# First block begun behind two quarters of the modulation, its columns in a fixed order, and small sums packed in column groups

## The chip, the core and the metric

The kernel runs on one core of a Trainium2 chip. The core has five engines, each with an instruction queue of its own: TensorE (PE) multiplies matrices and writes to PSUM banks, VectorE (DVE) and ScalarE (ACT) do element work, GpSimd (POOL) does small element work here, and SyncE (SP) issues the transfers (DMA) between the core's memory and HBM. Engines wait for one another through semaphores. The metric is the time of one execution on the device, in microseconds (us), lower is better; a time is the median of several executions.

## The reference

One layer of a diffusion backbone runs over 128 context tokens and 2048 latent tokens of width 1024. What the change touches is the beginning of the layer:

```
m = silu(cond) @ w_mod + b_mod                   # six vectors of 1024 for context and latent
h = rmsnorm(x, norm_mix) * (1 + sc1) + sh1       # modulated norm of the tokens
proj = h @ w_in                                  # q, k, v, gate, alpha/beta, u, vg
qkv = silu(centred_conv(proj[..., :1536], conv)) # three taps over neighbouring tokens
q, k = l2norm(q), l2norm(k)
beta2 = sigmoid(ab[..., 0]); g2 = -exp(a_log) * softplus(ab[..., 1] + dt_bias)
```

`ab`, the alpha and beta columns, are 16 of the 3088 columns of `w_in`. Behind it come a gated DeltaNet scan in two directions, a spatial gating, an output projection, a second modulated norm and an MLP.

## The kernel before

**Tiles and stages.** The 2176 tokens are 17 tiles of 128, in six blocks (`BLOCKS`): five of three tiles and a last one of two. Phase one goes over the blocks. The width 1024 is eight slices of 128, numbered `k` (`KT` = 8). A token block is kept transposed, features on the partitions, and split in two float32r halves, high and low, so that a product is three matrix products (`mm3`, L242 to L244): high by high, low by high, high by low.

**The modulation.** The first two of the six vectors are wanted at once. They are loaded as four quarters of eight loads of 256 KB (`mod_load`, L345): m0 and m2 are the halves of the shift, m1 and m3 those of the scale. `mod_sum` (L349) multiplies each slice's two columns of `scond` by the raw weights, in float32 and eight products in a row; `mod_out` (L358) turns the two rows into columns and makes `b1` (shift) and `a1` (scale and norm weight). Chunk `jc` = 4 of the later modulation is made by `split_mod_steps` (L372): each weight slice is split by ACT (a cast) and DVE (a subtraction) and multiplied with `abW`. The other chunks (`mod_steps`, L251) run on DVE, with a small packed sum at L281 at their end: there four products with two columns each go to PSUM partitions 0, 32, 64 and 96.

**A block.** `prep_block` (L446) yields steps: loading its x tiles, and one `column(k)` for each slice. For block 0 a column is three transposes on PE (L515), the modulation on ACT into `full` (L517), a cast to `kH` and a subtraction to `kL` on DVE (L520, L521), edge columns copied by POOL (L507 to L511) and four stores. Later blocks make `full` from transposed x on DVE (L527), `kH` on ACT and `kL` on DVE. The edges come from `xh`, the ten rows beside the block borders, normalised and modulated by `first_half` (L438) into `halH` and `halL`.

**A feature tile.** `feature_tile(blk, bi, gi, h)` (L545) is one of twelve in a block: group 1 is k, 0 is q, 2 is v, with four heads each. `project` does 24 products over the eight slices into a bank (`pj`, three of them; in block 0 one tile uses `pt`), then the convolution on ACT and DVE, then transposes back to tokens with squares for the norm (`to_tokens`, L582), back to features (L610) and the products of k and q (L620). `ab_block` (L638) multiplies the block's `kH` and `kL` with `abW`, which holds high and low halves of the alpha/beta weights (16 products), and transposes the 32 rows.

**What sets the order.** The kernel is written as lists of steps (`main` and `side`) which `interleave` merges; a scheduler then orders each engine's queue by its own estimate of times, within the dependences. `MOD_STEPS` says how many modulation steps go beside each tile of block 0. In block 0 (from L761 on) three k tiles are begun together on the first four columns; the fourth quarter is summed in between. Pools are rings of buffers: a new tile waits until an old one's last reader is done (`wp` has 49 of 2 KB on each partition, `full` two).

## Time and profile before

| | us |
|---|---|
| median of three executions | 2586.35 (2584.51 to 2587.87) |
| the profiled execution | 2589.03 |
| its span, first to last instruction | 2587.1 |
| PE busy in it | 2547.4 |
| PE busy from 0 to 100 us | 96.00 |
| first product of block 0 | at 36.87 |

The profile is one execution. Busy times are by engine; a row of the timeline gives start, length, engine, line, operation, what it writes and reads, its shapes and how many there are, and in brackets how long the engine stood idle before it and what ended that. A row of the table of stretches gives the stretch, its length and then, for PE, PE's weight loads (PEld), DVE, ACT and POOL, the busy time and (x) the instructions; then the granted clock of PE as a share of full speed, the mean share of the DMA engines and GB/s. A float32 product shows as two records. Rows of the chain of waits give start, length and what the chain that ended last went through.

### The profile page before, as it was taken

To read this page: it belongs to the slowest core of one execution; us is meant where nothing else is said; L and a number is where in the kernel's file an instruction comes from. 1 tells how busy PE (TensorE), PEld (TensorE's weight loads), DVE (VectorE), ACT (ScalarE), POOL (GpSimd) and SP (SyncE) were. 2 spreads that over 40 slices of the span, in tenths; PEclk is the share of its full clock that TensorE was granted. 3 is DMA by queue.
4 is the path that set the end of the run, shared out by engine and by line. 5 is a ranking of instruction groups with operands and counts; after the bars stand their busy time and mean duration, and the time that the engine had idled before them with its cause. 6 is when DMAs were issued, how large, how long until landed. Compare 5 with 4: busy or idle time off the path is not lost.

```text
span 2587.1 us, 44754 instructions
## 1 busy us (share of the span) xinstructions
PE 2547.4 (98%) x15556; PEld 2154.5 (83%) x15556; DVE 1805.3 (70%) x3738; ACT 1221.0 (47%) x3051; POOL 233.7 (9%) x448
## 2 busy tenths in 40 slices
PE   9999999999999999999999999999999999999998
PEld 5899998788888787788888888888888888888887
DVE  5867757766677878886678876666665557784875
ACT  4755556555555667764345543333342432342442
POOL 3112212111111111210000000000000000000000
PEclk9999999999999999999999999999999999999999
DMA  8977737644454656885868788444479979786683
GB/s 287 300 219 213 211 111 253 229 154 155 144 160 151 215 177 235 281 275 183 280 205 252 230 289 293 122 115 118 120 239 368 345 257 327 266 257 204 223 266 112
DMA packets 494695, 571.88 MB, mean 221 GB/s; under 512 B 35124, under 2 KB 297564, under 8 KB 490886
## 3 DMA queue, kind: packets, MB, share of 16 engines
q1 hardware_dynamic: 494470, 569.04, 67.8%
q8 instruction: 122, 2.00, 0.3%
q14 instruction: 103, 0.84, 0.1%
HBM read 389.23 MB, written 179.67 MB: 220 GB/s over the span
## 4 chain that ended last, share of the span: by engine, by line
PE 86%; DMA 6%; DVE 5%; ACT 2%; issue 1%; SPq 0%; POOL 0%; POOLq 0%; DVEq 0%; ACTq 0%
PE f L242 16%; PE f L244 16%; PE f L243 16%; PE pj L242 7%; PE pj L244 6%; PE pj L243 6%; PE pd L1011 4%; PE f L1646 2%; PE pm L242 1%; PE pm L244 1%; PE pm L243 1%; PE pt L626 1%; DMA QK<-qk_d 1%; DMA raw<-in_w_mod_dram 1%; DMA hop_d<-opL 1%
## 5 line engine op out<-in xcount | busy, mean ns | idle before, releaser
L242 PE MATMUL f<-hop,zH 128*128 128x512 f32 (+1 forms) x976 | 376.2, 386 | 1.2 <-ACT zH L1532 1.2
L243 PE MATMUL f<-hop,zH 128*128 128x512 f32 (+1 forms) x976 | 376.1, 386 | 0.0
L244 PE MATMUL f<-hop,zL 128*128 128x512 f32 (+1 forms) x976 | 376.1, 386 | 0.0
L242 PE MATMUL f<-hop,wH 128*128 128x512 f32 x896 | 355.2, 397 | 0.1
L243 PE MATMUL f<-hop,wH 128*128 128x512 f32 x896 | 349.0, 390 | 0.0
L244 PE MATMUL f<-hop,wL 128*128 128x512 f32 x896 | 347.9, 390 | 0.0
L1532 ACT CAST zH<-zraw 128x512 fp32r<-128x512 f32 x240 | 146.4, 620 | 284.6 <-DMA zraw<-s_d 86.9
L242 PEld LDWEIGHTS f<-hop,zH 128*128 128x128 f32 x976 | 183.3, 188 | 38.5 <-ACT zH L1532 1.6
L244 PEld LDWEIGHTS f<-hop,zL 128*128 128x128 f32 x976 | 183.3, 188 | 37.3 <-DVE zL L1526 0.4
L243 PEld LDWEIGHTS f<-hop,zH 128*128 128x128 f32 x976 | 183.3, 188 | 36.9 <-issue 0.2
L1526 DVE TENSOR_TENSOR zL<-zraw,zH 128x512 fp32r<-128x512 f32 x240 | 162.6, 687 | 72.2 <-ACT zH L1532 55.1
L244 PEld LDWEIGHTS f<-hop,wL 128*128 128x128 f32 x896 | 168.2, 188 | 35.3
L242 PEld LDWEIGHTS f<-hop,wH 128*128 128x128 f32 x896 | 168.5, 188 | 32.8 <-issue 0.5
L243 PEld LDWEIGHTS f<-hop,wH 128*128 128x128 f32 x896 | 168.5, 188 | 32.3
L242 PE MATMUL pj<-kH,wH 128*128 128x386 f32 (+2 forms) x568 | 190.5, 338 | 1.3 <-ACT junk L602 1.1
L243 PE MATMUL pj<-kL,wH 128*128 128x386 f32 (+2 forms) x568 | 189.5, 335 | 0.5 <-POOL kL L511 0.5
L244 PE MATMUL pj<-kH,wL 128*128 128x386 f32 (+2 forms) x568 | 189.7, 335 | 0.0
L185 POOL TENSOR_TENSOR r<-rsq,nhalf 128x1 f32<-128x1 f32 (+1 forms) x37 | 25.1, 679 | 1418.0 <-DVE rsq L184 1418.0
L572 DVE SCALAR_TENSOR_TENSOR cv<-pj,vec,cv 128x384 f32<-128x384 f32 (+2 forms) x164 | 87.0, 539 | 52.7 <-ACT cv L569 51.4
L242 PEld LDWEIGHTS pj<-kH,wH 128*128 128x128 f32 x568 | 107.0, 189 | 4.6 <-issue 2.6
L1532 ACT CAST wH<-s 128x512 fp32r<-128x512 f32 x96 | 59.4, 621 | 105.5 <-DVE s L1526 103.5
L243 PEld LDWEIGHTS pj<-kL,wH 128*128 128x128 f32 x568 | 107.4, 189 | 1.4 <-POOL kL L511 0.8
(410 smaller groups left out, 5703.9 us busy)
## 6 DMA issues: line engine op xcount, KB each, us to landing
zraw<-z_d SPq DMA_DIRECT2D x212, 256.0 KB
raw<-in_w_ff_dram SPq DMA_DIRECT2D x128, 256.0 KB
hop<-hop_d SPq DMA_DIRECT2D x28, 1024.0 KB
z_d<-c SPq DMA_DIRECT2D x96, 256.0 KB
zraw<-s_d SPq DMA_DIRECT2D x96, 256.0 KB
raw<-in_w_mod_dram SPq DMA_DIRECT2D x80, 256.0 KB
r<-in_w_ff_dram SPq DMA_DIRECT2D x80, 256.0 KB
s_d<-s SPq DMA_DIRECT2D x64, 256.0 KB
```

The lines of the kernel that those rows point to most:

```text
L185: G.tensor_tensor(out=out, in0=t[:np_, :n], in1=nhalf[:np_, :n], op=ALU.pow)
L242: T.matmul(ps, lh, rh, start=first and i == 0, stop=False, skip_group_check=more)
L243: T.matmul(ps, lh, rl, start=False, stop=False, skip_group_check=more)
L244: T.matmul(ps, ll, rh, start=False, stop=last and i == n - 1, skip_group_check=more)
L572: V.scalar_tensor_tensor(out=cv[:, o : o + m], in0=ps[:, s + sh : s + sh + m], scalar=convw[:, w, j : j + 1], in1=cv[:, o : o + m], op0=AL ...
L626: T.matmul(ps[:, i * P : (i + 1) * P], kTt[:, i * P : (i + 1) * P], rhs[:, i * P : (i + 1) * P], start=True, stop=True)
L1011: T.matmul(p[:, h, :], lhs[:, h, :], rhs[:, h, :], start=True, stop=True)
L1526: V.tensor_tensor(out=out, in0=a, in1=b, op=op)
L1532: A.copy(h, src)
L1646: T.matmul(ps[:, c : c + P], self.raw[m, kh][:, kp, :], x0[kh][:, kp, :], start=first and kp == 0, stop=last and kp == 3)
```

## The change

Quarters m0 and m1 are summed first, and then block 0 begins on columns 0 to 3 with four k tiles; m2 and m3 are summed between its slices (before slices 2 and 3), and columns 4 to 7 follow. The loads of x, the alpha/beta weights, the first two weight groups, m2 and m3 are issued in one chain on SP (`in_order`), and later loads of modulation and third weight group are put behind it (`follow`). PE's, DVE's and ACT's instructions from m1's sum to the end of slice 5 are chained in program order. `keep_on` puts 16 products of ones on PE behind m0's sum and 16 more behind the first edges. `first_half` works on four slices at once.

`groups` packs a sum over the eight slices: slice k goes to partitions 32 (k mod 4) of one bank, with 32 columns of `abW`, which now is float32 and holds alpha/beta in columns 0 to 15 and `scond` in 16 and 17. `sel` adds the four groups up in a further product. The four quarters, chunk 4, alpha/beta and a new `abias` (the shift's part of alpha/beta, for blocks 1 to 5) go through it. Alpha/beta is summed from `full` in float32, in two halves behind columns 3 and 7, so `full` has five buffers. The masks take another pool's room, and the zero edges of block 0 are written at the start.

```diff
-MOD_STEPS = (1, 1, 0, 0, 0, 1, 0, 2, 0, 1, 1, 2)
+MOD_STEPS = (0, 0, 0, 0, 1, 1, 0, 2, 1, 1, 2, 2)
...
-        abW = p1.tile([P, KT, P], F32R, tag="abW", name="abW", bufs=1)
-        V.tensor_copy(abW, zcol.unsqueeze(2).to_broadcast([P, KT, P]))
-        V.tensor_copy(abW[:, :, 32:34], scond)
-        V.tensor_tensor(out=abW[:, :, 64:66], in0=scond, in1=f32(abW)[:, :, 32:34], op=ALU.subtract)
+        abW = p1.tile([P, KT, 32], F32, tag="abW", name="abW", bufs=1)
+        V.memset(abW, 0.0)
+        V.tensor_copy(abW[:, :, 16:18], scond)
+        sel = p1.tile([P, 18], F32, tag="sel", name="sel", bufs=1)
+        V.tensor_tensor(out=sel, in0=ident[:, 0:18], in1=ident[:, 32:50], op=ALU.add)
+        for g in (64, 96):
+            V.tensor_tensor(out=sel, in0=sel, in1=ident[:, g : g + 18], op=ALU.add)
+        abias = p1.tile([P, 1], F32, tag="abias", name="abias", bufs=1)
+
+        def groups(ps, ks, moving):
+
+            for k in ks:
+                g = 32 * (k % 4)
+                T.matmul(ps[g : g + 32], abW[:, k, :], moving[k], start=k < 4, stop=k >= 4)
...
-            for k in range(KT):
-                T.matmul(pm[0:2, :], scond[:, k, :], raws[k], start=k == 0, stop=k == KT - 1)
-            row = pf.tile([2, 512], F32, tag="first", name="first", bufs=2)
-            A.copy(row, pm[0:2, :])
+            groups(pm, range(KT), raws)
+            row = pf.tile([P, 512], F32, tag="first", name="first", bufs=2)
+            A.copy(row, pm)
             return row
...
             for i in range(4):
-                T.transpose(pc[:, 2 * i : 2 * i + 2], row[:, i * P : (i + 1) * P], ident[0:2, 0:2])
+                T.matmul(pc[:, 2 * i : 2 * i + 2], row[:, i * P : (i + 1) * P], sel[:, 16:18], start=True, stop=True)
...
+                load(out=u[k], in_=w_mod[0, k * P : (k + 1) * P, jc * 512 : (jc + 1) * 512])
+                follow(start, loaded, mybir.EngineType.SP)
...
+                if i == 0:
+                    fetch(0), fetch(1), fetch(2), fetch(3)
+                elif i == 1:
+                    fetch(4), fetch(5)
+                elif i == 3:
...
+                    groups(u["ps"], range(4), u)
+                    in_order(begin, mybir.EngineType.PE)
+                    fetch(6), fetch(7)
+                    u["row"] = p1.tile([2, 512], F32, tag="mrow", name="mrow", bufs=1)
+                    load(out=u["row"], in_=b_mod[0:1, jc * 512 : (jc + 1) * 512].to_broadcast([2, 512]))
+                elif i == 6:
+                    groups(u["ps"], range(4, KT), u)
+                    in_order(begin, mybir.EngineType.PE)
+                    u["four"] = pf.tile([P, 512], F32, tag="first", name="four", bufs=2)
+                    A.copy(u["four"], u["ps"])
+                elif i == 7:
+                    ps = pm1()
+                    T.matmul(ps[0:2, :], sel[:, 16:18], u["four"], start=True, stop=True)
+                    V.tensor_tensor(out=u["row"], in0=ps[0:2, :], in1=u["row"], op=ALU.add)
+                    store(out=mod_d[:, jc * 512 : (jc + 1) * 512], in_=u["row"])
...
+        def follow(start, before, engine):
+
+            for x in tc.nc.cur_bb.bb.instructions[start:]:
+                if x.engine == engine:
+                    tc.add_manual_dep(x, before.name, mybir.DependencyInfo(
+                        mybir.DependencyClass.NoSync, mybir.DependencyReason.DATA), reason="order")
...
+        def in_order(start, *engines):
+
+            rows = tc.nc.cur_bb.bb.instructions
+            for e in engines:
+                own = [x for x in rows if x.engine == e]
+                at = len(own) - sum(x.engine == e for x in rows[start:])
+                for x, y in zip(own[max(at - 1, 0):], own[max(at, 1):]):
+                    tc.add_manual_dep(y, x.name, mybir.DependencyInfo(
+                        mybir.DependencyClass.NoSync, mybir.DependencyReason.DATA), reason="order")
...
+        def keep_on(n):
+
+            start, before = here(), last()
+            for _ in range(n):
+                T.matmul(warm[:, P : 2 * P], ones, ones, start=True, stop=True)
+            follow(start, before, mybir.EngineType.PE)
+
+        make_masks(pf.tile([P, 6, P], F16, tag="x2", name="one6", bufs=4))
+        edges = []
+        for k in range(KT):
+            pair = [p1.tile([P, 388], F32R, tag="h", name=n, bufs=24) for n in ("kH", "kL")]
+            for t in pair:
+                G.tensor_copy(t[:, 0:1], zcol[:, 0:1])
+                G.tensor_copy(t[:, 129:131], zcol[:, 0:2])
+            edges.append(pair)
...
         m0 = mod_load(0, 0)
         load(out=vec, in_=v_columns)
         convw = vec[:, 32:68].rearrange("p (w a) -> p w a", w=3)
+        xh = pf.tile([P, D], F32, tag="xh", name="xh", bufs=1)[0:10, :]
+        load(out=xh[0:8, :], in_=x_sample[0, 255 : 255 + 4 * 384, :].rearrange("(m r) d -> m r d", r=384)[:, 0:2, :])
+        load(out=xh[8:10, :], in_=x_sample[0, 255 + 384 * 4 : 257 + 384 * 4, :])
         m1 = mod_load(0, D)
+        start = here()
+        xs0 = []
+        for t in BLOCKS[0]:
+            x = p1.tile([P, D], F32, tag="x", name="x", bufs=3)
+            load(out=x, in_=xrow(t))
+            xs0.append(x)
+        abr = p1.tile([P, KT, 16], F32, tag="abr", name="abr", bufs=1)
+        load(out=abr, in_=w_ab)
+        w1a = load_w1(1, range(4))
+        m2 = mod_load(1, 0)
+        m3 = mod_load(1, D)
+        w1b = load_w1(1, range(4, KT))
+        wr = load_w1(0, range(KT))
+        in_order(start, mybir.EngineType.SP)
+        loaded = last()
         r0 = mod_sum(m0, pm1)
+        keep_on(2 * WARM)
+        pinned = here()
         r1 = mod_sum(m1, pj)
-        m2 = mod_load(1, 0)
+        def first_half(half):
+            ks = slice(half * 4, half * 4 + 4)
+            for tab, op in ((a1, ALU.mult), (b1, ALU.add)):
+                V.tensor_tensor(out=hal[:, ks, :], in0=hal[:, ks, :], in1=tab[:, 1, ks].unsqueeze(2)
+                                .to_broadcast([P, 4, 10]), op=op)
+            V.tensor_copy(halH[:, ks, :], hal[:, ks, :])
+            V.tensor_tensor(out=halL[:, ks, :], in0=hal[:, ks, :], in1=f32(halH)[:, ks, :], op=ALU.subtract)
+
         mod_out(r0, 0, b1, vec[:, 0:8], False)
...
-        r2 = mod_sum(m2, pj)
         norm_rows(xh)
...
-        xs0 = []
-        for t in BLOCKS[0]:
-            x = p1.tile([P, D], F32, tag="x", name="x", bufs=3)
-            load(out=x, in_=xrow(t))
-            xs0.append(x)
+        mod_out(r1, 0, a1, vec[:, 8:16], True)
+        first_half(0)
+        in_order(pinned, mybir.EngineType.PE, mybir.EngineType.DVE, mybir.EngineType.Activation)
+        keep_on(2 * WARM)
+        pinned = here()
         for x in xs0:
             norm_rows(x)
...
-                full = p1.tile([P, 384], F32, tag="full", name="full", bufs=2)
-                kH = p1.tile([P, 388], F32R, tag="h", name="kH", bufs=24)
-                kL = p1.tile([P, 388], F32R, tag="h", name="kL", bufs=24)
+                full = p1.tile([P, 384], F32, tag="full", name="full", bufs=5)
+                fulls[k] = full[:, :n]
+                if bi == 0:
+                    kH, kL = edges[k]
+                else:
+                    kH = p1.tile([P, 388], F32R, tag="h", name="kH", bufs=24)
+                    kL = p1.tile([P, 388], F32R, tag="h", name="kL", bufs=24)
...
+            def ab_sums(half):
+
+                if half == 0:
+                    sums["ps"] = pm1()
+                groups(sums["ps"][:, :n], range(4 * half, 4 * half + 4), fulls)
+                if half:
+                    sums["sb"] = sb = p1.tile([P, 384], F32, tag="absb", name="absb", bufs=1)
+                    if bi:
+                        V.tensor_scalar_add(sb[:, :n], sums["ps"][:, :n], abias)
+                    else:
+                        V.tensor_copy(sb[:, :n], sums["ps"][:, :n])
+
+            def ab_tokens():
+
+                pa = pt()
+                for i in range(len(tiles)):
+                    T.matmul(pa[:, i * 16 : (i + 1) * 16], sums["sb"][:, i * P : (i + 1) * P], sel[:, 0:16], start=True,
+                             stop=True)
+                V.tensor_copy(ab[:, tiles[0] : tiles[0] + len(tiles), :],
+                              pa[:, : len(tiles) * 16].rearrange("p (a b) -> p a b", b=16))
+
+            def column_sums(k, sums=True):
+                column(k)
+                if k % 4 == 3 and sums:
+                    ab_sums(k // 4)
+
...
+        def ab_bias():
+
+            ps = pm1()
+            groups(ps[:, 0:1], range(KT), [b1[:, 1, k : k + 1] for k in range(KT)])
+            V.tensor_copy(abias, ps[:, 0:1])
...
-        mods = [st for jc in range(4, 10) for st in (split_mod_steps(jc) if jc == 4 else mod_steps(jc, p1))]
+        mods = [st for jc in range(4, 10) for st in (group_mod_steps(jc) if jc == 4 else mod_steps(jc, p1))]
...
-        m3 = mod_load(1, D)
-        wr = load_w1(1, range(4))
-        mod_out(r1, 0, a1, vec[:, 8:16], True)
-        r3 = mod_sum(m3, pm1)
-        mod_out(r2, 1, b1, vec[:, 0:8], False)
-        W1[1] += [split_w(r) for r in wr]
-        first_half(0)
-        abr = p1.tile([P, KT, 16], F32, tag="abr", name="abr", bufs=1)
-        load(out=abr, in_=w_ab)
-        wk = load_w1(1, range(4, KT))
-        wr = load_w1(0, range(KT))
-        us = [feature_tile(blk, 0, 1, h) for h in range(3)]
-        for k in range(4):
-            cols[k]()
-            for u in us:
+        us = [feature_tile(blk, 0, 1, h) for h in range(4)]
+        cols[0](False)
+        W1[1].append(split_w(w1a[0]))
+        cols[1](False)
+        W1[1].append(split_w(w1a[1]))
+        for k in range(6):
+            if k == 3:
+                r3 = mod_sum(m3, pm1)
+                V.tensor_copy(abW[:, :, 0:16], abr)
+            for n, u in enumerate(us):
                 u["main"][k]()
-        mod_out(r3, 1, a1, vec[:, 8:16], True)
-        W1[1] += [split_w(r) for r in wk]
-        first_half(1)
-        for k in range(4, KT):
-            cols[k]()
-        V.tensor_copy(abW[:, :, 0:16], abr)
-        V.tensor_tensor(out=abW[:, :, 16:32], in0=abr, in1=f32(abW)[:, :, 0:16], op=ALU.subtract)
+                if n == 1 and k == 2:
+                    mod_out(r2, 1, b1, vec[:, 0:8], False)
+                if n == 1 and k == 3:
+                    mod_out(r3, 1, a1, vec[:, 8:16], True)
+                    first_half(1)
+                    cols[4](False)
+                    W1[1].append(split_w(w1b[0]))
+            if k == 1:
+                r2 = mod_sum(m2, pm1)
+            if k < 2:
+                cols[k + 2](False)
+                W1[1].append(split_w(w1a[k + 2]))
+            if k > 2:
+                cols[k + 2](False)
+                W1[1].append(split_w(w1b[k - 2]))
+            if k == 4:
+                blk[5](0)
+        blk[5](1)
+        in_order(pinned, mybir.EngineType.PE, mybir.EngineType.DVE, mybir.EngineType.Activation)
...
+        def third(k):
+            start = here()
+            raw = raw_w(w_in[0, k * P : (k + 1) * P, 1024:1536], sp, "raw")
+            follow(start, loaded, mybir.EngineType.SP)
+            W1[2].append(split_w(raw))
...
             if bi == 0:
-                order = [(1, 0), (1, 1), (1, 2), (0, 0), (0, 1), (1, 3), (0, 2), (0, 3)]
+                order = [(1, 0), (1, 1), (1, 2), (1, 3), (0, 0), (0, 1), (0, 2), (0, 3)]
...
-                main = u["main"][4:] if bi == 0 and n < 3 else u["main"]
+                main = u["main"][6:] if bi == 0 and n < 4 else u["main"]
...
-                if n == 1:
-                    ab1, ab2 = ab_block(blk, bi)
-                    side.append(ab1)
+                if bi == 0 and n == 1:
+                    side.append(ab_bias)
                 if n == 2:
-                    side.append(ab2)
+                    side.append(blk[4])
```

93 lines of the change are left out of this document (29 added, 64 removed).

## The prediction

> **What bounds the kernel now.** I read the page first (busy times, then the chain that ended last), then the table of stretches over the first 100 us, then TensorE's timeline there.
>
> ```profile
> PE 2547.4 (98%) x15556; PEld 2154.5 (83%) x15556; DVE 1805.3 (70%) x3738; ACT 1221.0 (47%) x3051; POOL 233.7 (9%) x448
> PE 86%; DMA 6%; DVE 5%; ACT 2%; issue 1%; SPq 0%; POOL 0%; POOLq 0%; DVEq 0%; ACTq 0%
> ```
>
> TensorE (PE) is busy for 98% of the span. So a microsecond is won where PE's own work shrinks or where PE is busy without getting on, and an idle PE has only 40 us to give in all. The start is the place of the second kind:
>
> ```profile
> 4.95 8.25 PE L353 MATMUL pm<-raw,scond 128*2 128x512 f32 x16
> 17.75 7.89 PE L353 MATMUL pj<-raw,scond 128*2 128x512 f32 x18
> 36.87 0.62 PE L242 MATMUL pj<-kH,wH 128*128 128x388 f32 x2
> 59.24 0.34 PE L242 MATMUL pj<-kH,wH 128*128 128x388 f32 x1
> 59.42 0.34 PE L243 MATMUL pj<-kL,wH 128*128 128x388 f32 x1
> ```
>
> The four modulation sums (L353) hold PE from 4.95 us until the first product of block 0 at 36.87: 8.25 us for a sum whose product appears as two records, so about 1 us a product. From there products follow one another every 0.18 us (59.24 to 59.42; I use 0.178).
>
> ```profile
> 49.53 0.45 PE L243 MATMUL pj<-kL,wH 128*128 128x388 f32 x1 [0.46 <-POOL kL L511]
> 70.67 0.52 PE L585 MATMUL pt<-ident,x 128*128 128x128 f32 x3 [0.76 <-DVE ab L657]
> 72.34 0.52 PE L585 MATMUL pt<-ident,x 128*128 128x128 f32 x3 [0.28 <-DVE x L576]
> 73.99 0.41 PE L242 MATMUL pj<-kH,wH 128*128 128x388 f32 x1 [1.13 <-ACT junk L602]
> 70.00:80.00 10.00, 7.93 (x46) 7.42 (x47) 9.31 (x27) 10.00 (x37) 1.27 (x2) 1.00 1.02 348
> ```
>
> After that PE stands 0.46 us once and 2.2 us around 72 us, where ACT is busy for all 10 us of its window (fourth engine column). There is little else to win in block 0.
>
> **When block 0 starts after the change.** The first product now needs quarters m0 and m1 alone, but it stands at the end of a chain that is pinned in program order on PE, DVE and ACT. Its links:
>
> ```profile
> 5.70 10.94 SPq L191 DMA_DIRECT2D raw<-in_w_mod_dram  x16
> 11.12 5.17 DMA raw<-in_w_mod_dram
> 20.53 0.57 ACT L355 COPY first<-pj 2x512 f32<-2x512 f32 x1 [6.72 <-PE pj L353]
> 22.89 1.05 ACT L336 ACTIVATE junk<-xh 10x1024 bf16<-10x1024 f32 x1 [1.78 <-DMA xh<-in_x_sample_dram]
> 25.54 0.13 DVE L184 TENSOR_SCALAR rsq<-ss 128x1 f32<-128x1 f32 x1
> 25.75 0.56 POOL L185 TENSOR_TENSOR r<-rsq,nhalf 128x1 f32<-128x1 f32 x1 [0.92 <-DVE rsq L184]
> 26.34 0.75 DVE L338 TENSOR_SCALAR x<-x,r 128x1024 f32<-128x1024 f32 x1 [0.67 <-POOL r L185]
> 27.72 0.66 PE L420 MATMUL pt<-ident,xh 10*128 10x10 f32 x8
> 29.52 0.23 DVE L421 COPY hal<-pt 128x80 f32<-128x80 f32 x1
> 156.70 0.67 PE pt L626 x6
> 28.03 0.22 DVE L369 SCALAR_TENSOR_TENSOR a<-a,vec 128x4 f32<-128x4 f32 x2
> 33.45 0.91 ACT L517 ACTIVATE full<-pt,b,a 128x128 f32<-128x128 f32 x2 [3.82 <-PE pt L515]
> ```
>
> The load issued at about 11.1 us, the sixteenth of 256 KB by SP's pace of 0.68 us (10.94/16), landed at 16.3; the two xh loads now ahead of m1 add some 0.6: 16.9. Then: last packed product 0.95 (17.85), copy of the sums 0.57 (18.4), square of xh 1.2 with its read-out (19.6), rsq, POOL's power and the scaling 1.55, that is 25.54 to 27.09 (21.2), xh's transposes and copy 0.9 (22.1), four 128-wide float32 products with sel at 0.22 each by L626's row (three products in 0.67) 0.9 (23.0), three small DVE steps 0.5 (23.5), four of first_half 0.7 at that pace (24.2). Only now may DVE take up the three x tiles, since its order is pinned, and each waits for POOL in turn: 3 x 1.55 = 4.65 (28.8). Transposes 0.33, ACT's pair 0.91, DVE's second cast 0.3: 30.4, with handovers **30.5 us**. Block 0 starts 6.4 us earlier. DMA doesn't bind: at 0.68 us a load, x, w_ab, four of w1, m2 and m3 have landed by 35, and their sums come behind it. If the chain of DVE were free, the last x tile (21 us) would give 25.3; if xh's small loads cost double, 31.1. The 16 filler products (keep_on, 3.6 us) end near 26.6 and hide behind this chain.
>
> **What block 0 then carries.** I compare the time at which the 96 products of tiles (1,0) to (1,3), the eight columns and the alpha/beta sums are through.
>
> ```profile
> 151.74 0.55 PE pm L281 x16
> 152.29 0.37 PE pj L242
> 152.66 0.17 PE pj L243
> 154.25 0.33 PE pt L585 x3
> 194.55 0.30 PE pt L654 x3
> 43.69 5.67 POOL L510 CAST kH<-halH 128x1 fp32r<-128x1 f32 x4 [8.83 <-DVE halH L443]
> L510 POOL CAST kH<-halH x32: 178/180/4917, 31.7 to 111.0; 128x1 fp32r<-128x1 f32 x32
> L520 DVE CAST kH<-full x16: 215/254/295, 33.9 to 51.7; 128x128 fp32r<-128x128 f32 x8, 128x256 fp32r<-128x256 f32 x8
> L202 ACT CAST wH<-raw x32: 606/622/787, 35.5 to 96.3; 128x512 fp32r<-128x512 f32 x32
> L203 DVE TENSOR_TENSOR wL<-raw,wH x32: 677/684/693, 36.2 to 96.9; 128x512 fp32r<-128x512 f32 x32
> ```
>
> L281 already packs columns: eight 128-wide products (16 records) pass in 0.55 us, against 8 x 0.22 one by one, 3.2 times as fast; the next product took 0.37, not 0.18, so a switch of tile shape costs 0.19. A 384-wide float32 product alone takes 0.75 x 0.99 = 0.74 us (0.99 is 7.89/8). Eight packed are 1.5 us if four lie wholly side by side, 1.85 at 3.2 times; I take 1.6, and 2.0 for 512 wide.
>
> Before: 36.87 + 96 x 0.178 (17.1) + 16 alpha/beta products (2.85) + seven columns' transposes at 0.33 (2.3) + four small transposes (0.4) + the 0.46 stall = 60.0. After: 30.5 + 17.1 + six columns (2.0) + the sums of m2 and m3 (4.0) + their collection with sel (1.8) + alpha/beta (1.6) + four switches (0.8) = 57.8, and four waits that the fixed order puts on PE:
> - wL of the first weight comes 0.4 late, behind column 0 on DVE.
> - Column 4 needs mod_out(r3) and first_half(1) first: about 0.8 beyond the products that cover it.
> - The sixth `full` finds no buffer (five) until ab_sums(0), which stands behind k = 4 on PE; then ACT's pair and DVE's cast, 1.5, and wL 0.5: 2.0. Nothing else can run on PE: three pj banks and the pt bank are held.
> - POOL's edge casts of columns 4 to 7. One took 4.9 us of the 5.67, while DVE had no gap. Between 0.2 and 4.9 us; behind the pinned order DVE has a gap after column 4 and its wL (two casts, two subtractions, 0.68), so I take 1.5.
>
> Sum 62.5: this stage **loses 2.5 us** although it starts 6.4 earlier; the range is from a gain of 3 (no waits but the first) to a loss of 6.
>
> **The rest of phase one.** Alpha/beta in each later block: before 2.85 + 0.30 (L654) + 0.19 (the product after L654 pays the switch too) = 3.34. After: 1.6 + two switches 0.38 + three products with sel 0.67 = 2.65. Four blocks at 0.7 and the two-tile block at 0.5: **3.3 us gained** (0 to 5). abias' eight one-column products fit in a wait of block 0. Chunk jc = 4: 16 products of 0.178 x 512/388 = 0.235 (3.8) become 2.0 + 0.99 + 0.38 = 3.4, 0.4 gained; its eight casts and eight subtractions go from ACT and DVE. These, 0.62 and 0.68 each, stood at 35 to 97 us; of the 2.2 us stall near 72 I count 0.7 as gained (0 to 2.2), as most of ACT's load there (convolutions, squares, W1 casts) stays. The sums' bank moves from pj to pm, and junk goes into a tile that ACT alone writes; both free something and I count nothing. Masks and zero edges move on POOL to before the first loads have landed. On SP the kH/kL stores, the third weight group and block 1's x tiles now queue behind the pinned loads, whose last lands near 43; the x tiles can't start before column 7 frees their buffers anyway. MOD_STEPS only moves side steps by a tile or two. Later phases keep their PE work and shift.
>
> Sum: -2.5 + 3.3 + 0.4 + 0.7 = 1.9 us gained. The profiled execution took 2589.03 us (2587.1 of span and 1.9 around it) and would take 2587.1; it lay 2.7 above the median of 2586.35, to which I refer the forecast: **2584.5 us**. About 0.2%, 5.2 us, is what a measurement of this kernel can tell from no change.
>
> **Rivals.**
> - *The waits are covered* (0.33). The edge casts cost nothing (1.5), the buffer wait is half (1.0), the stall at 72 goes wholly (1.5 more), packing is complete (0.1 to 0.25 in each of six blocks and two sums, 1.5), and the start is 2 us earlier because xh's norm overlaps. For it: DVE stood only 70% busy. Against: the order is pinned. 7.5 more: 2577.
> - *PE waits at the moved sums* (0.15), the slower side. Today's alpha/beta products run in tile n = 1, with all kH long written; ab_sums(1) now sits at a block's end, behind column 7.
>
> ```profile
> L527 DVE SCALAR_TENSOR_TENSOR full<-xT,a,rrow x40: 464/610/619, 88.3 to 380.4; 128x384 f32<-128x384 f32 x32, 128x256 f32<-128x256 f32 x8
> 104.00:112.00 8.00, 7.57 (x48) 7.21 (x46) 7.18 (x15) 5.62 (x17) 6.77 (x28) 1.00 1.03 326
> ```
>
>   Four columns there are eight such DVE steps, 4.9 us, in a tile of 24 x 0.178 = 4.3 us of PE, and DVE is 90% busy around that edge (7.18 of 8). At 1.6 us a boundary, five times, 8 us: 2592.5. It decides from 0.4 us a boundary, where the 1.9 is gone.
> - *The clock drops before block 0* (0.08). PE has little but six transposes between 26.6 and 30.5.
>
> ```profile
> L353 PE MATMUL pm<-raw,scond x32: 589/592/1057, 4.9 to 36.3; 128*2 128x512 f32 x32
> ```
>
>   A record at the cold start took 1057 ns, not 592. If products ran at half pace for as long as the filler lasts, 3.6 us, 1.8 us go: 2586.3. The Trainium skill (TensorE: Matmul & The Clock Gate, "What's actually happening") says that PE falls to half its clock after an idle window of about 3.4 us; by that rule a gap of 3.9 us could just do it, while the trace before has no such gap to show it.
> - *Packing fails at these widths* (0.03): eight products of 0.74 one by one cost 4.3 more in six blocks: about 2610.
>
> **How the numbers follow.** The forecast's case has 0.41, 2580 to 2589. Faster by over 5.2 us: the first rival (0.33) and the forecast's best edge (0.03). Slower: the moved sums (0.13 of 0.15), the last rival and a block 0 that loses 6 (0.02). The range from 2572 to 2593 takes in the first rival's case, and the slow one to its middle.
>
> **What would show it.** First L242 at 30 to 31 us; a PE wait on DVE `full` or kH before k = 5, and on POOL before k = 4, around 45 to 52; 0.7 to 0.9 us for each half of the alpha/beta sums; PE's idle time at block edges. Wrong would be: a start by 26, PE without gaps in 30 to 60, or waits at L527's readers in every block.

## The result: slower by 0.55%, and the profile after

The changed kernel takes 2600.77 us (median of six runs, 2597.49 to 2602.08) against 2586.92 us (2583.26 to 2587.87) for the kernel before beside it: a ratio of 1.0055, 95% interval 1.0045 to 1.0066, some 13.9 us slower. The forecast was 2584.5, the range 2572 to 2593. The profiled execution after took 2597.49 us, with a span of 2595.7 us.

From the page of the changed kernel, the busy times and the chain that ended last:

```profile
PE 2550.4 (98%) x15671; PEld 2157.1 (83%) x15671; DVE 1802.3 (69%) x3720; ACT 1218.4 (47%) x3044; POOL 222.6 (9%) x432
PE 3%; DMA 1%; DVE 1%; ACT 0%; issue 0%; POOL 0%; POOLq 0%; SPq 0%; ACTq 0%
```

Neither row shows the loss: TensorE is at 98% before and after, and the chain of this execution can be followed back over only some 5% of the span, so its shares can't be set beside those of before. The stretches of the first 105 us do. First the kernel before, then the changed one; the columns are the busy time of PE, PEld, DVE, ACT and POOL, then the granted clock of PE, the DMA share and GB/s:

```profile
0.00:30.00 30.00, 28.62 (x85) 9.01 (x86) 7.20 (x40) 7.71 (x13) 14.38 (x72) 1.00 0.88 302
30.00:45.00 15.00, 15.00 (x71) 8.96 (x71) 11.80 (x44) 9.47 (x20) 4.71 (x27) 1.00 0.92 313
45.00:60.00 15.00, 14.54 (x85) 14.13 (x84) 12.17 (x33) 9.04 (x20) 5.05 (x7) 1.00 0.81 261
60.00:75.00 15.00, 12.84 (x75) 11.81 (x74) 8.17 (x22) 8.95 (x25) 0.78 (x1) 1.00 0.96 321
75.00:90.00 15.00, 15.00 (x87) 14.39 (x86) 14.77 (x37) 14.30 (x49) 3.75 (x4) 1.00 0.74 215
90.00:105.00 15.00, 15.00 (x97) 14.61 (x96) 11.28 (x26) 10.63 (x34) 1.98 (x9) 1.00 1.02 299
```

```profile
0.00:30.00 30.00, 25.79 (x137) 17.97 (x137) 8.52 (x42) 7.16 (x12) 14.72 (x79) 0.89 0.90 318
30.00:45.00 15.00, 11.62 (x65) 8.84 (x63) 7.45 (x21) 5.90 (x13) 0.85 (x2) 0.89 1.04 382
45.00:60.00 15.00, 12.97 (x96) 9.35 (x96) 6.79 (x27) 4.94 (x11) 1.95 (x8) 0.96 0.85 258
60.00:75.00 15.00, 11.92 (x53) 9.92 (x53) 11.34 (x26) 10.30 (x23) 0.00 (x0) 0.84 0.77 230
75.00:90.00 15.00, 13.82 (x82) 13.38 (x81) 13.38 (x32) 12.22 (x41) 0.94 (x2) 0.97 0.72 226
90.00:105.00 15.00, 11.47 (x60) 9.56 (x61) 15.00 (x33) 7.55 (x25) 3.67 (x3) 0.89 0.70 204
```

Two things are new in every row: TensorE is busy for less (87.6 us of the 105 against 101.0), and the granted clock has a mean of 0.84 to 0.97 in place of 1.00. Between 30 and 60 us VectorE and ScalarE are less busy than before, too, so neither is out of capacity there: they wait as well.

TensorE's timeline of the changed kernel names the places; the bracket is the idle time before the row and what ended it:

```profile
24.45 5.61 PE L452 MATMUL pt<-ones 128*128 128x128 f32 x32
...
31.14 0.33 PE L590 MATMUL pt<-ident,x 128*128 128x128 f32 x1 [0.97 <-DVE rsq L184]
...
32.62 0.66 PE L590 MATMUL pt<-ident,x 128*128 128x128 f32 x4 [1.15 <-DVE x L338]
34.51 0.41 PE L242 MATMUL pj<-kH,wH 128*128 128x388 f32 x1 [1.23 <-ACT wH L202]
...
41.20 1.92 PE L353 MATMUL pm<-raw,abW 128*32 128x512 f32 x16
...
56.00 0.85 PE L353 MATMUL pm<-full,abW 128*32 128x384 f32 x8
...
58.40 0.44 PE L242 MATMUL pj<-kH,wH 128*128 128x388 f32 x1 [1.45 <-ACT wH L202]
...
72.30 0.41 PE L242 MATMUL pj<-kH,wH 128*128 128x388 f32 x1 [3.08 <-DVE cv L674]
...
93.53 0.66 PE L242 MATMUL pj<-kH,wH 128*128 128x388 f32 x1 [4.71 <-DVE rsq L184]
```

Block 0 starts at 34.51, not 30.5. The grouping does what was forecast: eight products 512 wide in 1.92 us, against 8.25 for the same number of records before (0.23 of it), a half of alpha/beta in 0.85. The long waits, 3.08 and 4.71 us, are both for a pj bank, behind the stage that the prediction worked out. (At 93.53 the row names `rsq`, VectorE's last small step; the convolution's step that reads the bank, L674, ended 0.08 us before it.)

Where TensorE's time up to the 288th product went (the last of block 0; 108.36 us before, 130.05 after) is worked out from its rows: from each start to the next, with the idle time taken out.

| us on TensorE up to the 288th product | before | after | |
|---|---|---|---|
| modulation sums (m0 to m3, jc = 4) | 33.5 | 15.4 | -18.1 |
| the products of block 0 | 52.8 | 61.4 | +8.6 |
| fillers | 3.7 | 12.7 | +9.0 |
| collections, alpha/beta to tokens | 1.6 | 5.9 | +4.3 |
| alpha/beta sums and bias | 2.8 | 4.8 | +2.0 |
| transposes and key products of side steps | 9.9 | 12.4 | +2.6 |
| idle | 2.8 | 16.2 | +13.4 |
| sum | 107.1 | 128.8 | +21.7 |

The grouping frees 18.1 us, and nothing comes of it: fillers (9.0), idle time (13.4) and products at half pace (most of the 8.6) take more than that. Some of the +2.0 and +2.6 is work of block 1 and of side steps that is merely done sooner.

### The profile page after: what moved, and what is told of

Its sections match the earlier page's. It is cut to its first block, busy times and chain, and to the rows that moved or that the text cites. A ratio compares the mean times of both kernels' runs of the same rounds, so it can differ in the third digit from the quotient of the medians.

```text
span 2595.7 us, 44911 instructions
## 1 busy us (share of the span) xinstructions
PE 2550.4 (98%) x15671; PEld 2157.1 (83%) x15671; DVE 1802.3 (69%) x3720; ACT 1218.4 (47%) x3044; POOL 222.6 (9%) x432
## 3 DMA queue, kind: packets, MB, share of 16 engines
q1 hardware_dynamic: 494466, 569.04, 67.6%
## 5 line engine op out<-in xcount | busy, mean ns | idle before, releaser
L243 PEld LDWEIGHTS f<-hop,zH 128*128 128x128 f32 x976 | 183.3, 188 | 38.2 <-DVE hop L1623 1.2
L244 PEld LDWEIGHTS f<-hop,zL 128*128 128x128 f32 x976 | 183.3, 188 | 36.9 <-DVE zL L1623 0.4
L1623 DVE TENSOR_TENSOR zL<-zraw,zH 128x512 fp32r<-128x512 f32 x240 | 162.8, 687 | 65.4 <-ACT zH L1629 53.8
L674 DVE SCALAR_TENSOR_TENSOR cv<-pj,vec,cv 128x384 f32<-128x384 f32 (+2 forms) x164 | 87.0, 539 | 57.7 <-ACT cv L671 56.5
L244 PEld LDWEIGHTS pj<-kH,wL 128*128 128x128 f32 x568 | 109.0, 192 | 2.1 <-DVE wL L203 1.1
```

The costliest lines, as they stand in the source:

```text
L243: T.matmul(ps, lh, rl, start=False, stop=False, skip_group_check=more)
L244: T.matmul(ps, ll, rh, start=False, stop=last and i == n - 1, skip_group_check=more)
L674: V.scalar_tensor_tensor(out=cv[:, o : o + m], in0=ps[:, s + sh : s + sh + m], scalar=convw[:, w, j : j + 1], in1=cv[:, o : o + m], op0=AL ...
L1623: V.tensor_tensor(out=out, in0=a, in1=b, op=op)
```

## The experiments

The milestones below are starts of the nth product of phase one and the end of the last one (1728th), read from TensorE's rows; "rest" is from there to the end of the span. Times are us; the ratio is to the kernel before on the same chip. The two profiles of the changed kernel, which is the same in both, differ by 4.2 us at the 96th product and by 1.4 to 1.8 elsewhere in phase one: smaller differences between two rows can be chance.

| kernel | ratio [95%] | 1st | 96th | 192nd | 288th | 432nd | end of phase one | rest |
|---|---|---|---|---|---|---|---|---|
| before | 1 | 36.9 | 61.2 | 82.7 | 108.4 | 145.9 | 428.3 | 2158.8 |
| before, second profile | 1.0003 [0.9992, 1.0014] | 35.8 | 60.8 | 83.5 | 109.1 | 145.0 | 427.4 | 2156.4 |
| changed | 1.0055 [1.0045, 1.0066] | 34.5 | 68.9 | 101.5 | 130.1 | 161.9 | 439.7 | 2156.0 |
| changed, second profile | 1.0062 [1.0038, 1.0086] | 33.1 | 64.7 | 99.8 | 128.3 | 160.2 | 438.0 | 2160.0 |
| e1_modlate | 1.0042 [1.0029, 1.0056] | 34.4 | 68.7 | 95.1 | 124.3 | 153.7 | 435.0 | 2157.2 |
| e2_tileends | 1.0067 [1.0053, 1.0081] | 33.8 | 66.7 | 98.5 | 128.4 | 158.9 | 440.2 | 2163.6 |
| e3_pool | 1.0066 [1.0053, 1.0078] | 31.4 | 63.0 | 103.8 | 133.7 | 163.9 | 442.7 | 2160.8 |
| f1_all | 1.0033 [1.0020, 1.0046] | 32.1 | 65.3 | 90.3 | 120.0 | 151.1 | 430.9 | 2157.3 |
| x4_pack | 1.0000 [0.9991, 1.0009] | 37.2 | 59.8 | 80.4 | 107.7 | 144.6 | 426.2 | 2158.3 |
| g2_fill | 1.0038 [1.0025, 1.0050] | 31.9 | 63.8 | 89.6 | 117.8 | 150.6 | 432.1 | 2164.1 |
| h1_squares | 1.0040 [1.0027, 1.0053] | 32.9 | 64.5 | 96.8 | 126.6 | 157.1 | 435.9 | 2159.0 |
| c0_nofill | 1.0086 [1.0072, 1.0100] | 35.5 | 68.4 | 98.5 | 135.1 | 165.3 | 445.8 | 2166.8 |
| u1_late | 1.0081 [1.0068, 1.0094] | 39.2 | 66.3 | 102.4 | 132.3 | 162.8 | 443.4 | 2166.4 |
| u2_late | 1.0021 [1.0012, 1.0030] | 38.2 | 65.6 | 89.7 | 119.4 | 150.9 | 431.0 | 2159.3 |
| h2_all | 1.0042 [1.0029, 1.0054] | 31.9 | 63.8 | 88.1 | 119.8 | 149.3 | 430.1 | 2163.0 |

### The modulation steps between the convolutions (e1_modlate)

The changed kernel's VectorE ahead of the wait at 93.53:

```profile
86.49 0.74 DVE L272 SCALAR_TENSOR_TENSOR acc<-raw,scond,acc 128x512 f32<-128x512 f32 x1
87.16 0.34 DVE L674 SCALAR_TENSOR_TENSOR cv<-pj,vec,cv 128x128 f32<-128x128 f32 x1
88.09 0.75 DVE L272 SCALAR_TENSOR_TENSOR acc<-raw,scond,acc 128x512 f32<-128x512 f32 x1 [0.59 <-DMA raw<-in_w_mod_dram]
88.76 0.35 DVE L674 SCALAR_TENSOR_TENSOR cv<-pj,vec,cv 128x128 f32<-128x128 f32 x1
89.02 0.74 DVE L272 SCALAR_TENSOR_TENSOR acc<-raw,scond,acc 128x512 f32<-128x512 f32 x1
```

An accumulation of chunk jc = 5 (L272, 0.74 us) stands between every one or two steps of a convolution (L674), and one waits for its own load with the convolutions behind it. In the kernel before these steps came only from 104 us on; there chunk jc = 4 held the `raw` buffers with its split weights, and the change gave those buffers up. That the freed buffers let the steps in is argued from the code: no run separates it from the other changes of the order.

```diff
+        def held(st):
+            def g():
+                start = here()
+                st()
+                for e in (mybir.EngineType.DVE, mybir.EngineType.SP):
+                    follow(start, convs[-1], e)
+            return g
...
-                side += mods[:nm]
+                side += [held(st) if bi < 2 and len(mods) - i <= 40 else st for i, st in enumerate(mods[:nm])]
```

> The changed kernel, with the modulation steps of chunk jc = 5 and later in blocks 0 and 1 held on VectorE and SyncE behind the latest convolution in program order. Theory: in block 0 these accumulations (0.67 to 0.74 us each, two to a slice) stand between the convolutions, so a pj bank comes free late: the wait of 4.71 us at 93.5 us goes, and with it some 1 us of half clock behind it. About 5.5 us faster than the changed kernel, near 2595. Rival (the loss made there is given back later anyway, since block 1 and the scan already regain some 13 of the 22 us): the milestone at the end of block 0 moves by 5 us and the end by under 2, near 2600. Second rival (the bank is late because the convolutions themselves are late, whatever stands between them): the wait stays, within 1 us of the changed kernel.

TensorE's waits between 30 and 130 us, first of the changed kernel, then of this one:

```profile
PE pj L242 <- DVE rsq L184: 4.7, 1, 4.7
PE pj L242 <- DVE cv L674: 3.1, 1, 3.1
```

```profile
PE pj L242 <- DVE cv L675: 3.1, 1, 3.1
PE pj L242 <- ACT wH L202: 2.7, 2, 1.4
```

The wait of 4.7 is gone, the others stay. The 192nd product comes 6.4 us earlier, the end of phase one 4.7 (3.0 against the second profile of the changed kernel). Not all of the first gain is kept: the steps held back must be done later, and from the 432nd product to the end of phase one this kernel takes 281.3 us, the changed one 277.8. By the ratios it is 3.4 us faster (0.0013 x 2587), with intervals that overlap. The theory stands. The second rival falls; of the first a part is true.

### Tile ends one by one (e2_tileends)

```diff
+        pinned = here()
+        for u in us:
+            u["main"][6]()
+            u["main"][7]()
+        in_order(pinned, mybir.EngineType.PE)
...
-                main = u["main"][6:] if bi == 0 and n < 4 else u["main"]
+                main = [] if bi == 0 and n < 4 else u["main"]
```

> The changed kernel, with slices 6 and 7 of the four key tiles of block 0 chained on TensorE tile by tile, so that the tiles end one after the other and not all at about 69 us. Theory: the wait of 3.08 us for a pj bank at 72.3 us comes from four tiles that end together and ask for all their convolutions at once; it goes, with about 1.5 us of half clock behind it: 3 to 4.5 us faster than the changed kernel, near 2597. Rival (the convolutions and the weight splits on VectorE and ScalarE are the bound of this stretch, not their bunching): the wait only moves to a later bank, less than 1 us is gained.

TensorE's timeline of this kernel:

```profile
68.33 0.41 PE L242 MATMUL pj<-kH,wH 128*128 128x388 f32 x1 [1.28 <-DVE cv L674]
...
89.04 0.67 PE L242 MATMUL pj<-kH,wH 128*128 128x388 f32 x1 [5.76 <-DVE rsq L184]
```

The first wait shrinks from 3.08 to 1.28, as the theory has it (it is 3.08 in both profiles of the changed kernel and in e1_modlate). The next one is 5.76 us, 4.71 and 5.67 in the two profiles of the changed kernel; ahead of it an accumulation waits 2.00 us for its load on VectorE:

```profile
84.25 1.42 DVE L272 SCALAR_TENSOR_TENSOR acc<-raw,scond,acc 128x512 f32<-128x512 f32 x2 [2.00 <-DMA raw<-in_w_mod_dram]
```

The end of phase one doesn't move. The rival is right as to the time; that bunching had a part in the first wait is shown.

### GpSimd in order (e3_pool), and what stood behind it (h1_squares)

The start of block 0 in the changed kernel, GpSimd and VectorE:

```profile
25.82 0.70 POOL L585 CAST kH<-halH 128x1 fp32r<-128x1 f32 x5 [4.88 <-DVE halH L494]
...
27.10 1.01 POOL L586 CAST kL<-halL 128x1 fp32r<-128x1 f32 x4
...
29.61 0.18 POOL L586 CAST kL<-halL 128x1 fp32r<-128x1 f32 x1
29.75 0.55 POOL L185 TENSOR_TENSOR r<-rsq,nhalf 128x1 f32<-128x1 f32 x1
...
30.34 0.75 DVE L338 TENSOR_SCALAR x<-x,r 128x1024 f32<-128x1024 f32 x1 [2.32 <-POOL r L185]
```

PE, DVE and ACT were pinned, GpSimd was not. As soon as halH and halL exist, its one-column casts of the edges, some of block 1 among them, go ahead of the power that VectorE needs for x.

```diff
-        in_order(pinned, mybir.EngineType.PE, mybir.EngineType.DVE, mybir.EngineType.Activation)
+        in_order(pinned, mybir.EngineType.PE, mybir.EngineType.DVE, mybir.EngineType.Activation,
+                 mybir.EngineType.Pool)
...
+                if bi:
+                    follow(start, convs[-1], mybir.EngineType.Pool)
```

> The changed kernel, with GpSimd's queue held in program order too in block 0, and the edge casts of later blocks held behind the latest convolution. Theory: the power for the rows of the first x tiles (0.55 us) stands behind some twenty one-column casts that the planner drew ahead of it; in order, VectorE's wait of 2.32 us before the scaling of x goes, and the first product of block 0 comes at about 32.5 us, not 34.5. 2 to 3 us faster than the changed kernel, near 2598. Rival (block 0 is bound by VectorE and ScalarE from its first slices on): the first product comes 2 us earlier, the 96th at the same 68.9, and the end doesn't move.

The first product comes at 31.4, 3.1 us earlier, the 96th 5.9 earlier (1.7 against the second profile), and then everything is lost. ScalarE and TensorE of this kernel:

```profile
68.29 1.06 ACT L539 ACTIVATE junk<-x 128x1024 bf16<-128x1024 f32 x1 [7.03 <-DMA x<-in_x_sample_dram]
...
69.34 0.97 ACT L675 ACTIVATE cv<-pj,vec 128x128 f32<-128x128 f32 x3
...
72.61 0.67 PE L242 MATMUL pj<-kH,wH 128*128 128x388 f32 x1 [9.29 <-DVE cv L678]
```

ScalarE stands for 7.03 us at the square of an x tile of block 1 that hasn't landed (its load was issued at 64.2, behind the key stores on SP), the convolutions behind it in ScalarE's queue, and TensorE 9.29 us behind those. The next kernel holds that square back as well:

```diff
                 A.activation(junk, x, AF.Square, accum_out=xs[0][:, i : i + 1])
+                if bi == 1:
+                    follow(start, acts[-1], mybir.EngineType.Activation)
...
-                    side += nxt[1][n : n + 1]
+                    if bi:
+                        side += nxt[1][n : n + 1]
+                    elif n >= 3:
+                        side += nxt[1][n - 3 : n - 2]
```

> The changed kernel with GpSimd's queue in order (as in the third experiment), and the loads and squares of block 1's x tiles begun three tiles later and held on ScalarE behind the convolutions made by then. Theory (in the third experiment ScalarE stood 7.03 us at a square whose x tile had not landed, with the convolutions behind it in its queue, and TensorE 9.29 us for the pj bank that they free): that wait goes, and the end of phase one comes 6 to 9 us earlier than in that experiment, at 434 to 437 us. Rival (the convolutions were late for another reason): a wait of several us for a pj bank stays between 60 and 75 us. A third way: the later squares make block 1's columns late, and the wait comes back at its start.

Phase one ends at 435.9, 6.8 us earlier than in the kernel without it and in the range expected. Waits of 2.8 us (at 67.6, a pj bank) and 3.2 us (at 87.4, a transpose) remain, so of the rival, which has a pj wait of several us between 60 and 75, a part is true.

### All three (f1_all), with fillers (g2_fill), with everything (h2_all)

> The changed kernel with all three edits. Theory: the three losses are at different places and add up: 10 to 12 us faster than the changed kernel, 2589 to 2591, about 2 to 4 us over the kernel before. Rival (they share one bound, the work of VectorE and ScalarE in the first 130 us): less than the largest of the three alone plus 1 us.

The kernel has the three edits shown so far: the steps held, the tile ends, GpSimd in order. Phase one ends at 430.9, 8.8 us earlier than in the changed kernel, where the first edit alone gave 4.7 and the two others lost 0.4 and 2.9: the waits of 3.1 and 4.7 are both gone, and that of the third experiment too. Against the second profile of the changed kernel it is 7.1 us. By the ratio the gain is 5.7 us, short of the 10 to 12 expected.

```diff
             if k == 4:
                 blk[5](0)
+                keep_on(6, pm1())
```

> The three edits together, and six filler products on TensorE behind the first half of the alpha/beta sums of block 0, where TensorE stands idle for 1.5 us and the products behind it are 0.325 us apart instead of 0.178. Theory (the idle time there makes the clock fall, and the clock costs as much as the wait): the fillers lie in the wait, the ten or so slow products behind it run at 0.178 again, and the 96th product comes 1.5 us earlier, at 63.8 instead of 65.3. Rival (the clock falls for another reason, the packed products themselves or the whole stretch before): the products behind the wait stay slow and the 96th comes at 65 or later.

The 96th product comes at 63.8, as expected, and TensorE of this kernel shows the fillers in the place of the wait and the products behind it at 0.18:

```profile
52.79 1.61 PE L452 MATMUL pm<-ones 128*128 128x128 f32 x12
...
55.68 0.34 PE L242 MATMUL pj<-kH,wH 128*128 128x388 f32 x1
55.86 0.34 PE L243 MATMUL pj<-kL,wH 128*128 128x388 f32 x1
```

But phase one ends no earlier (432.1 against 430.9): the 1.5 us are lost again at other waits. Nor is one profile enough for the clock here, as the last section shows.

> The three edits, the six fillers and the squares of block 1 held behind the convolutions, with the early start kept: the best version of the change that the theories give. Each of the known waits of the first 100 us is gone but those for the sixth full buffer and for column 4's casts: end of phase one at 427 to 430 us (428.3 before, 430.9 with the three edits), 2586 to 2590. Rival (every edit makes the planner order the free stretch anew, and a wait of 2 to 9 us turns up at another place in most of the orders): phase one ends at 432 or later in spite of the edits.

The end of phase one, 430.1, lies at the upper edge of the theory's range, 2 to 3 us behind the kernel before; the time, 2596.3 (a ratio of 1.0042), is above the 2586 to 2590 expected and no better than with the three edits.

### Without the second fillers (c0_nofill)

```diff
-        keep_on(2 * WARM)
         pinned = here()
         for x in xs0:
             norm_rows(x)
```

> The changed kernel without the second group of 16 filler products, which run from 24.5 us to the first transposes of block 0. Theory (the clock falls behind idle time): some 5 us of idle time stand in their place, the transposes and the first products of block 0 run at half pace for longer, and the first product comes at the same time or up to 0.5 us later; the 96th comes 1 to 2 us later. Rival (the fillers are themselves in the way of the chain, since the transposes wait for their end): the first product comes up to 1 us earlier.

By the ratio 8 us slower than the changed kernel. TensorE of this kernel at its first products:

```profile
37.15 0.53 PE L243 MATMUL pj<-kL,wH 128*128 128x388 f32 x1
37.48 0.53 PE L244 MATMUL pj<-kH,wL 128*128 128x388 f32 x1
```

They are 0.325 us apart. So they are in the first profile of the changed kernel, where the granted clock from 36 to 38 us is 0.50, and not in its second:

```profile
36.49 0.53 PE L244 MATMUL pj<-kH,wL 128*128 128x388 f32 x1
36.82 0.53 PE L242 MATMUL pj<-kH,wH 128*128 128x388 f32 x1
```

```profile
34.26 0.34 PE L242 MATMUL pj<-kH,wH 128*128 128x388 f32 x1
34.44 0.34 PE L243 MATMUL pj<-kL,wH 128*128 128x388 f32 x1
```

The first product comes 1.0 and 2.4 us later than in those two, more than the theory's 0.5; that the fillers keep the clock up is not shown. The 96th, at 68.4, lies between theirs (68.9 and 64.7), and the 192nd comes 1 to 3 us earlier. What is lost in phase one is lost between the 192nd and the 288th (36.5 us against 28.6), in this stretch:

```profile
105.00:130.00 25.00, 22.85 (x130) 19.00 (x131) 13.55 (x30) 13.53 (x46) 2.25 (x9) 0.86 0.75 221
```

The granted clock is 0.86 there, 1.00 in the changed kernel. This stretch lies some 75 us behind the place of the fillers, in the part that the planner orders anew; how much of the 8 us is theirs is open.

### The grouping of alpha/beta alone (x4_pack)

```diff
-        ps = (pj if bi else pm1)()
-        for k in range(KT):
-            T.matmul(ps[:, :ncol], abW[:, k, :], hH[k][:, :ncol], start=k == 0, stop=False)
-            T.matmul(ps[:, :ncol], abW[:, k, :], hL[k][:, :ncol], start=False, stop=k == KT - 1)
+        for k in ks:
+            g = 32 * (k % 4)
+            T.matmul(ps[g : g + 32], abP[:, k, :], fulls[k], start=k < 4, stop=k >= 4)
```

> The kernel before with one part of the change alone: alpha and beta in column groups (two halves of four products, the bias by a sum of its own, the collection with sel), and four full buffers instead of two. The first block, the modulation quarters and chunk jc = 4 stay as before. Theory (the grouping is worth what was forecast, the early start of block 0 is what costs): block 0 keeps its first product at 36.9 us, each block gains some 0.7 us, and the time is 3 to 4 us under the kernel before, a ratio of 0.9985 to 0.9990. Rival (the moved sums make TensorE wait at the block boundaries, so the grouping is part of the loss): not faster than before, waits for VectorE behind the columns at each boundary.

The groups of TensorE in this kernel from 36 to 430 us (96 records, six blocks):

```profile
L366 PE MATMUL pm<-full,abP 128*32 128x384 f32 (+1 forms) x96 | 13.7, 480 | 0.0
```

13.7/6 is 2.3 us a block by the lengths of the records (2.1 from start to start), not the 1.6 forecast. A half whose four products stay together takes 0.78 us from start to start, as forecast; in four of the five later blocks the planner sets other products between the four of a half, and each break costs some 0.6 to 0.8 us more. Phase one ends 2.2 us earlier than in the first profile before, 1.3 earlier than in the second; the ratio, 1.0000, can't tell 2 us. No wait at a block boundary is added, so the rival falls too: the grouping of alpha/beta costs nothing; the 1 to 2 us that it may bring are hardly more than the 0.9 and 1.7 us by which two profiles of one kernel differ.

### The early start undone (u1_late, u2_late)

```diff
         us = [feature_tile(blk, 0, 1, h) for h in range(4)]
+        r2 = mod_sum(m2, pm1)
+        r3 = mod_sum(m3, pm1)
+        mod_out(r2, 1, b1, vec[:, 0:8], False)
+        mod_out(r3, 1, a1, vec[:, 8:16], True)
+        first_half(1)
         cols[0](False)
...
```

> The changed kernel with the early start alone undone: the sums of the quarters m2 and m3, their collection and the second half of first_half stand ahead of column 0 again, and their loads ahead of those of the weights. Everything else of the change stays (grouping, fixed order, tile by tile of four, chunk jc = 4). Theory (what costs is that the stage of the first 96 products is interrupted: two sums of 1.92 us, two collections of 0.95 us, the wait for column 4's casts, and the clock that falls behind its idle time): the first product comes at 36 to 38 us, but the 96th at 60 to 63 instead of 68.9, and the end of phase one 3 to 6 us earlier, near 2595. Rival (the loss comes from what follows the fixed order, the free stretch from 69 us on, in which the planner's order doesn't fit): the 96th comes earlier, but the waits behind it grow by as much, and the end moves by less than 2 us.

Here our theory fell. TensorE's waits from 0 to 430 us in this kernel:

```profile
PE pj L242 <- DVE cv L674: 5.6, 1, 5.6
PE pj L242 <- DVE rsq L184: 4.8, 1, 4.8
```

The first product comes 4.7 us later and the 96th 2.6 earlier, so from the first to the 96th it takes 27.1 us in place of 34.4 (31.6 in the second profile): the interruptions, with the clock, cost some 4 to 7 us in that stage. But the wait behind it grows from 3.1 to 5.6, and phase one ends 3.6 us later. The rival holds as to the waits; the end, which it had within 2 us, comes later still.

> The same undoing of the early start, with the three edits (modulation steps of jc = 5 and later held, tiles ended one by one, GpSimd in order). If the early start is a loss of its own: under the three edits alone (2594, ratio 1.0033) by 3 to 6 us, at 2588 to 2591, and the first product at 35 to 37 us. If only the free stretch behind the fixed order counts: the same as the three edits alone.

With the three edits on both sides, the start at 38.2 or at 32.1 makes 0.6 us at the 192nd product (89.7 and 90.3) and 0.1 at the end of phase one (the ratios, 1.0021 and 1.0033, are 3 us apart with intervals that overlap). Six microseconds at the start are worth nothing there: what stands behind the pinned stretch sets the time.

### Is anything lost behind phase one (r_after, r_before)

> The changed kernel unaltered, for a second profile. What is open: in the first pair of profiles the changed kernel is 11.4 us behind at the end of phase one and 8.6 at the end of the span, while the medians differ by 13.9. Theory (the whole loss is made in phase one, and what comes behind it only varies from run to run by some 4 us): phase one ends at 438 to 442 us again, with the waits at 58, 72 and 93 us in their places, and from there to the end it takes the 2156 to 2161 us that the other runs show. Rival (the change costs something behind phase one too): more than 2162 us from there to the end, in this profile but not in that of the kernel before.

> The kernel before unaltered, for a second profile beside it: the first product at 36.9 us, phase one ends at 427 to 429 us; from there to the end 2155 to 2160 us by the theory.

Phase one ends at 438.0 against 427.4, a loss of 10.6 after 11.4 in the first pair. The rest takes 2156.0 and 2160.0 us in the changed kernel, 2158.8 and 2156.4 in the kernel before: no second loss in these pairs. The twelve profiles of the changed kernel and its variants have a mean of 2161.1 there, the three of before and x4_pack 2157.8, each with a spread of several us, so up to some 3 us behind phase one stay open. The second profile of the changed kernel also shows how little the stage up to the 96th product counts: 4.2 us earlier there (64.7), 1.7 from the 192nd on.

## Why the prediction was wrong

- **What bounds the kernel.** Right as far as it went: the start was "TensorE busy without getting on". The changed kernel frees 18.1 us of that. Drawn too short was the next step, that this time is to be had. While those sums ran, the profile's rows give a granted clock of 1.00, and the loads and the chain of the norms went on beside them. In their place the changed kernel has 9 us more of fillers and, in the first 30 us, a granted clock of 0.89.
- **The start at 30.5.** It came at 34.5 (33.1 in the second profile). The step "each waits for POOL in turn: 3 x 1.55" took GpSimd as free; the one-column edge casts in its queue were overlooked at this place. In the five kernels that have GpSimd in order and the early start it is 31.4 to 32.9.
- **The waits of the stage.** Of the right kind and mostly no larger than forecast: 0.44 for the casts of column 4 (1.5 forecast), 1.45 for the sixth `full` and its weight (2.0). The grouped sums and collections took 1.92, 0.95 and 0.85 as forecast. (One price was misread without deciding anything: the 7.89 us that it divides by eight are 18 records, nine products, so a product 512 wide took 0.88 us, not 0.99.) The 96th product at 68.9 instead of 62.5 (all sums included) is the start, 4.0 us later, and the clock, which costs the products 5.2 us in this profile; together more than the difference, as the other waits came out smaller. In the second profile the clock costs 2.3 and the 96th stands at 64.7.
- **The step that failed** is "of the 2.2 us stall near 72 I count 0.7 as gained", with "MOD_STEPS only moves side steps by a tile or two" beside it. Behind the fixed order the planner lays out the steps anew, and there the changed kernel waits 3.1 and 4.7 us (3.1 and 5.7 in the second profile) where the kernel before waits 2.2. From the 96th to the 192nd product it takes 32.6 and 35.1 us, the kernel before 21.5 and 22.7: where 0.7 us was to be gained, some 11 to 12 are lost, a part of which is work done sooner. The cause of the second wait is shown (e1_modlate: the steps of jc = 5 stand between the convolutions), that of the first in part (e2_tileends). The four kernels with these two edits and GpSimd in order (f1_all, g2_fill, u2_late, h2_all) have no wait over 1.3 us behind the fixed order and end phase one at 430.1 to 432.1; the other eight profiles of the changed kernel and its variants each have one of 2.8 us or more and end it at 435.0 to 445.8.
- **Alpha/beta in the later blocks, 3.3 gained.** From the 432nd product to the end of phase one the changed kernel takes 277.8 us against 282.4, alike in both profiles of each. But e1_modlate, with the modulation steps held back, takes 281.3 and x4_pack 281.6. So about 1 us seems to be the grouping, and the rest work that block 0 had done early. The term was sized by halves left whole; x4_pack has broken ones in four of the five later blocks.
- **The rivals.** "The clock drops" came true (0.08 was its chance), not once for 1.8 us but at four places of block 0, and for the fillers ahead of it, which took 5.61 us instead of 3.6 (granted clock 0.50 from 24 to 28 us). Products more than 0.25 us apart cost block 0 9.5 us over the usual 0.178, against 1.5 before; in the second profiles, with two such places in the changed kernel and one in the kernel before, 7.3 against 2.7. "PE waits at the moved sums" didn't: no boundary of blocks 1 to 5 has such a wait. "Packing fails" didn't at the quarters, and in part at alpha/beta.

What stays open: with the long waits edited away phase one still ends 2 to 5 us behind the kernel before, and none of the ten variants of the changed kernel is as fast as it (the best, u2_late, at 1.0021; the four with the three edits are 5 to 11 us slower by their ratios). So these edits account for some 6 to 10 us of the 11 lost in phase one, and for 3 to 9 of the 14 in the time; the cause of the rest is open. Each edit makes the planner order the free stretch anew; which part of a difference of 2 or 3 us is the edit and which the new order can't be told here.

## What to carry over

Time freed on a busy engine is worth only what the chain beside it can follow: ask what the freed engine waits for next, and whether its old work hid that. When an order is fixed on some engines, name the queue of every other engine that the fixed chain passes through, and look at the stretch behind it, where a planner may set a step that waits for its load ahead of the steps that free a bank. And freed buffers can let later work in: ask which, and between what it will stand.

## What the runs showed of the hardware

Behind idle time TensorE's products can come at 0.325 us instead of 0.178, while the granted clock is 0.50. In the changed kernel, behind the wait of 1.45 us:

```profile
60.11 0.52 PE L243 MATMUL pj<-kL,wH 128*128 128x388 f32 x1
60.43 0.53 PE L244 MATMUL pj<-kH,wL 128*128 128x388 f32 x1
60.00:62.00 2.00, 2.00 (x7) 2.00 (x7) 0.97 (x2) 0.00 (x0) 0.00 (x0) 0.50 0.85 253
```

Not behind every gap. Counting three or more products at that pace within 6 us as a drop, over the profiles of the table: of 13 gaps of 2.79 us or more in phase one, 11 are followed by one. At a twelfth, the 5.46 us of e3_pool, the granted clock falls to 0.50 as well (from 96 to 98 us), but the slow instructions are transposes; at the 2.79 us of h1_squares it stays at 1.00. Of ten gaps of 1.44 to 1.50 us, all at the same place of block 0, three are followed by a drop (the changed kernel, e1_modlate, f1_all), while the second profile of the unaltered changed kernel has the same gap and none; two more of that length stand just ahead of block 0 (u1_late, u2_late), both with a drop behind them. And the kernel before has a gap of 1.13 us near 73 us in both profiles; in the second the granted clock behind it is 0.50 from 74 to 76 us, in the first 1.00. So the fillers of g2_fill are not proved to have done it by that one profile. The Trainium skill (TensorE: Matmul & The Clock Gate, "What's actually happening") has the clock at half after an idle window of about 3.4 us. The three gaps of 3.08 us, each followed by a drop, agree with it roughly; the short ones show that a gap of a third to a half of that length can be followed by a drop as well, and what else decides it is open.
